# Sliding windows by DMA: twelve staged batches instead of eleven, direct copies in halves, a rebuilt end

## The chip, the cores and the metric

The kernel runs on one core of one Trainium2 chip. The metric is the device time of one execution in microseconds. The core has 16 DMA engines, which all its DMA queues share; the trace records every packet that they move, with its queue, size, start and duration.

## The reference

`x` has 32 batches of 4096 rows of 256 float32 values. Each batch is cut into windows of 64 rows, one every 32 rows, so 127 windows overlap by half:

```python
n_windows = (length - window_size) // stride + 1          # 127
result = np.zeros((batch, n_windows, window_size, dim), dtype=np.float32)
for i in range(n_windows):
    start = i * stride                                    # 32 * i
    result[:, i] = x[:, start:start + window_size].copy()
```

Nothing is computed, only copied: 134 MB in, 266 MB out. In units of a block (32 rows, 32 KB) a batch has 128 blocks, and window `w` is block `w` followed by block `w + 1`. Every block but the first and last of a batch is written twice.

## The kernel before, in words

All data is moved by DMA, on three queues. A batch goes one of two ways:

- **Direct** (21 batches): DRAM to DRAM. `Copier.windows` (L29) copies `n` windows; with `half=None` each window is one row of 64 KB, cut into pieces of at most 32 KB; with `half` 0 or 1 only the first or second block of each window is copied, one piece of 32 KB each. SyncE (SP, `ring_d`, queue q1 of the profile) issues them, 16 windows at a time, seven groups a batch.
- **Staged** (11 batches: 1, 4, 7, ... 31): `Staging.load` (L86) brings the 128 blocks of a batch into a tile of 128 partitions, 32 KB each, and `Staging.store` (L97) writes the tile out twice, once as the first halves of the windows and once as the second halves. ScalarE (ACT, `ring_s`, q10) issues them, in pieces of 16 KB. Six tiles are used in turn: six loads, then their twelve stores, then five loads that each wait for the tile's stores, then their stores (`run`, L116).

A staged batch's store writes all 128 blocks both times, so its first halves spill one block into the next batch's window 0, and its second halves one block into the window 126 of the batch before. Those windows belong to direct batches and are written again after the store has landed. These are the **edges** (L166): of the 127 windows of a direct batch, seven groups of 16 are 112, and the other 15, on the side of the staged neighbour, are left to GpSimd (POOL, `ring_r`, q0). POOL waits for the semaphore `near` (L192), which the group of q1 before the last one raises when it lands, then for the `stored` semaphore of each neighbour (L196), and issues the edges in order. The last staged batch, 31, is loaded one block early and stored in smaller parts (L103 to L110); the last direct batch, 30, ends with two `columns` DMAs (L200, L203) that cut windows into small rows spread over all engines.

What each queue gets is set ahead of time by a planner written into the loop (L171 to L187): it counts "turns" of the staged queue and sets, by stage, what share of the 16-window groups is issued as two halves and which as whole windows: 120 of 120 at the start and around the second loads, 90 of 120 while loads run, 18 of 120 otherwise. At the end SP waits for all semaphores (L206).

Each queue is a list in order: ACT's waits (tile free, tile loaded) hold back everything that ACT issues later, POOL's hold back later edges, and SP's later direct groups. The functions as they stand, with the profile's line numbers:

Of the kernel before, what the change touches and what calls it, by code (L numbers as in the profile page):

```python
# [8 lines left out]
DIRECT, IN, OUT = 32768, 16384, 16384  # L9


class Copier:


    def __init__(self, x, out, B, L, D, W, S, n_win):
        assert W == 2 * S and L % S == 0
        self.x, self.out = x, out
        self.B = B
        self.blk = S * D
        self.nb = L // S  # L20
        self.nw = n_win
# [18 lines left out]
    def columns(self, q, b, w0, n):  # L40
# [5 lines left out]
            in_=self.xap(b * self.nb + w0, [[part, 16], [self.blk, n], row]),  # L46
        )

    def load(self, q, t, b, c, rows):

        p, step, n, unit = rows
        return q.dma_start(
            out=t[p : p + (n - 1) * step + 1 : step, :],
            in_=self.xap(b * self.nb + c + p // unit, [[step // unit * self.blk, n], [1, self.blk]]),
            max_dma_last_dim=IN,
        )

    def store(self, q, t, b, c, rows, half):


        p, step, n, unit = rows
        w = b * self.nw + c + p // unit - half
        return q.dma_start(
            out=self.oap(2 * w + half, [[2 * step // unit * self.blk, n], [1, self.blk]]),
            in_=t[p : p + (n - 1) * step + 1 : step, :],
            max_dma_last_dim=OUT,
        )


class Staging:  # L70


    def __init__(self, c, tc, pool, dtype, items, bufs):
        self.c, self.items = c, items
        self.tiles = [pool.tile([128, c.blk], dtype, name=f"xb{i}") for i in range(bufs)]
        self.loaded = [tc.alloc_semaphore(f"loaded{i}") for i in range(bufs)]
        self.stored = [tc.alloc_semaphore(f"stored{i}") for i in range(bufs)]
        self.ended = tc.alloc_semaphore("ended")
        self.count = {sem: 0 for sem in (*self.loaded, *self.stored, self.ended)}
        self.after_load, self.after_store = {}, {}  # L80

    def issue(self, dma, sem):
# [2 lines left out]

    def load(self, q, g):  # L86
        i = g % len(self.tiles)
        b, c, n = self.items[g]
        if self.count[self.stored[i]]:
            q.wait_ge(self.stored[i], self.count[self.stored[i]])  # L90
        step = 128 // n
        parts = [(k, 4, 32, 1) for k in range(4)] if g == 0 else [(0, step, n, step)]
        for rows in parts:
            self.issue(self.c.load(q, self.tiles[i], b, c, rows), self.loaded[i])
        self.after_load[g] = self.count[self.loaded[i]]

    def store(self, q, g):  # L97
        i = g % len(self.tiles)
        b, c, n = self.items[g]
        q.wait_ge(self.loaded[i], self.after_load[g])  # L100
        step = 128 // n
        parts, end = [((0, step, n, step), 0), ((0, step, n, step), 1)], []
        if g == len(self.items) - 1:  # L103

            parts = [((0, 1, 128, 1), 1), ((0, 1, 32, 1), 0)]
            end = [(96, 1, 32, 1)] + [(32 + k, 4, 16, 1) for k in range(4)]
        for rows, half in parts:
            self.issue(self.c.store(q, self.tiles[i], b, c, rows, half), self.stored[i])
        for rows in end:
            self.issue(self.c.store(q, self.tiles[i], b, c, rows, 0), self.ended)  # L110
        self.after_store[g] = self.count[self.stored[i]]

    def wait_stored(self, q, g):
        q.wait_ge(self.stored[g % len(self.tiles)], self.after_store[g])  # L114
# [1 line left out]
    def run(self, q):  # L116
        bufs = len(self.tiles)
        for first in range(0, len(self.items), bufs):
            group = range(first, min(first + bufs, len(self.items)))
            for g in group:  # L120
                self.load(q, g)
            for g in group:
                self.store(q, g)


@with_exitstack
def kernel(
    ctx: ExitStack,
    tc: tile.TileContext,
    x: bass.AP,  # L130
    window_size: bass.AP,
    stride: bass.AP,
    out: bass.AP,
):
    nc = tc.nc
    W, S = int(window_size), int(stride)
    B, L, D = x.shape
    n_win = (L - W) // S + 1
    assert out.shape == (B, n_win, W, D)
    c = Copier(x, out, B, L, D, W, S, n_win)  # L140


    staged = [*range(1, B, 3)]
    items = [(b, -1 if b == B - 1 else 0, c.nb) for b in staged]
    place = {b: g for g, (b, _, n) in enumerate(items) if n == c.nb}
    direct = [b for b in range(B) if b not in staged]
    pool = ctx.enter_context(tc.tile_pool(name="xb", bufs=1))
    st = Staging(c, tc, pool, x.dtype, items, 6)
    ring_d, ring_s, ring_r = nc.sync, nc.scalar, nc.gpsimd
    done = tc.alloc_semaphore("done")  # L150
    near = tc.alloc_semaphore("near")
    rest = tc.alloc_semaphore("rest")
    total = {done: 0, near: 0, rest: 0}

    def count(dma, sem):
        dma.then_inc(sem, 16)
        total[sem] += 16

    sixteens = []
    for b in direct:
        w = 15 if b - 1 in staged else 0
        sixteens += [(b, w + 16 * j) for j in range((c.nw - w) // 16)]
    singles = [(B - 1, c.nw - 1, 1)]
    edges = [(b, 0 if b - 1 in staged else 112, 15) for b in direct[:-1]]  # L166
    last = B - 2
    edges.append((last, 112, 4))

    first_loads, loads, stores = 6 * 17, 5 * 17, 6 * 34  # L170
    turns = share = 0  # L171
    with tc.tile_critical():  # L172
        st.run(ring_s)

        for i, (b, w) in enumerate(sixteens):
            sem = near if i == len(sixteens) - 2 else done
            second = turns - first_loads - stores
            loading = turns < first_loads or 0 <= second < loads
            share += 120 if turns < 16 or -8 <= second < 16 else 90 if loading else 18
            if share >= 120:  # L180
                share -= 120
                turns += 4
                count(c.windows(ring_d, b, w, 16, 0), done)
                count(c.windows(ring_d, b, w, 16, 1), sem)
            else:
                turns += 3
                count(c.windows(ring_d, b, w, 16), sem)  # L187
            if i == len(sixteens) // 2:
                for b, w, half in singles:
                    count(c.windows(ring_d, b, w, 1, half, 2048), done)  # L190

        ring_r.wait_ge(near, 16)  # L192
        for b, w, n in edges:
            for k in (b - 1, b + 1):
                if k in place and b != last:
                    st.wait_stored(ring_r, place[k])  # L196
            count(c.windows(ring_r, b, w, n), rest)


        count(c.columns(ring_r, last, 116, 9), rest)  # L200
        ring_r.drain()  # L201
        st.wait_stored(ring_d, place[B - 1])
        count(c.columns(ring_d, last, 125, 2), done)  # L203
        total[st.ended] = st.count[st.ended]
        for sem, n in total.items():
            ring_d.wait_ge(sem, n)  # L206
# [35 lines left out]
```

## Time and profile before

| what | value |
|---|---|
| median of 3 runs | 754.74 us (751.68 to 755.06) |
| span of the profiled execution, first to last instruction | 742.1 us |
| bytes moved by the DMA engines | 313.26 MB, mean 422 GB/s |
| DMA packets | 18290, of these 4336 of 4 bytes (completions) |
| direct groups on SP | 92 of 1024 KB (whole windows), 110 of 512 KB (halves) |
| staged loads and stores on ACT | 10 loads and 21 stores of 4096 KB, and 10 smaller DMAs |
| POOL starts its first edge | at 649.1 us of the span |
| last DMA packet ends | at 739.7 us |

The profiled execution's own time is not listed apart from its span; the span lies 12.6 us below the median of the runs. Times in the text are in the span's clock. MB and GB/s of the DMA engines count a byte once when it is moved; HBM counts it when it is read and when it is written, so a direct copy is two HBM bytes a byte moved and a staged load or store is one. "Excess" is used for the time that packets take beyond the shortest time of their size.

### The profile page before, as it was taken

To read this page: it belongs to the slowest core of one execution; us is meant where nothing else is said; L and a number is where in the kernel's file an instruction comes from. 1 tells how busy PE (TensorE), PEld (TensorE's weight loads), DVE (VectorE), ACT (ScalarE), POOL (GpSimd) and SP (SyncE) were. 2 spreads that over 40 slices of the span, in tenths; PEclk is the share of its full clock that TensorE was granted. 3 is DMA by queue.
4 is the path that set the end of the run, shared out by engine and by line. 5 is a ranking of instruction groups with operands and counts; after the bars stand their busy time and mean duration, and the time that the engine had idled before them with its cause. 6 is when DMAs were issued, how large, how long until landed. Compare 5 with 4: busy or idle time off the path is not lost.

```text
span 742.1 us, 323 instructions
## 1 busy us (share of the span) xinstructions
POOL 12.7 (2%) x26
## 2 busy tenths in 40 slices
POOL 0000000000000000000000000000000000050100
DMA  8999999999999999999999999999999999999996
GB/s 361 424 430 427 435 431 428 423 435 425 428 427 426 428 428 420 429 435 427 427 427 412 433 435 431 427 436 432 434 424 429 430 424 426 428 435 432 421 420 253
DMA packets 18290, 313.26 MB, mean 422 GB/s; under 512 B 4336, under 2 KB 4336, under 8 KB 4528
## 3 DMA queue, kind: packets, MB, share of 16 engines
q1 hardware_dynamic: 8016, 154.32, 48.8%
q10 hardware_dynamic: 9104, 138.41, 44.0%
q0 software_dynamic: 1168, 20.51, 6.6%
q14 instruction: 2, 0.02, 0.0%
HBM read 220.95 MB, written 267.09 MB: 658 GB/s over the span
## 4 chain that ended last, share of the span: by engine, by line
another core or an unknown queue 92%; POOL 2%; issue 0%; POOLq 0%; SPq 0%
POOL out_dram L34 2%; POOLq L201 0%; POOLq L237 0%; SPq L172 0%; POOLq L114 0%
## 5 line engine op out<-in xcount | busy, mean ns | idle before, releaser
L34 POOL DMA_DIRECT2D out_dram<-in_x_dram x21 | 12.0, 575 | 685.4 <-DMA out_dram<-in_x_dram 648.7
L44 POOL DMA_DIRECT2D out_dram<-in_x_dram x1 | 0.6, 581 | 0.0
L223 POOL MEMSET const-float32-0.0<- 128x1 f32 x1 | 0.1, 98 | 0.2 <-issue 0.2
L223 POOL MEMSET const-bfloat16-1.0<- 128x1 bf16 x1 | 0.1, 101 | 0.0
L223 POOL MEMSET const-float32-1.0<- 128x1 f32 x1 | 0.1, 98 | 0.0
L223 POOL MEMSET const-uint8-127<- 128x1 uint8 x1 | 0.1, 98 | 0.0
## 6 DMA issues: line engine op xcount, KB each, us to landing
out_dram<-in_x_dram SPq DMA_DIRECT2D x92, 1024.0 KB, 99.8
out_dram<-xb ACTq DMA_DIRECT2D x21, 4096.0 KB, 138.5
out_dram<-in_x_dram SPq DMA_DIRECT2D x110, 512.0 KB, 90.2
xb<-in_x_dram ACTq DMA_DIRECT2D x10, 4096.0 KB, 130.5
out_dram<-in_x_dram POOLq DMA_DIRECT2D x20, 960.0 KB, 37.9
xb<-in_x_dram ACTq DMA_DIRECT2D x4, 1024.0 KB, 15.7
out_dram<-xb ACTq DMA_DIRECT2D x2, 1024.0 KB, 110.5
out_dram<-xb ACTq DMA_DIRECT2D x4, 512.0 KB, 94.4
```

Of the source, the lines that this page charges most:

```text
L34: return q.dma_start(out=self.oap((b * self.nw + w0) * 2 + h, [[2 * blk, n], row]), in_=self.xap(b * self.nb + w0 + h, [[blk, n], row]), m ...
L44: return q.dma_start(out=self.oap((b * self.nw + w0) * 2, [[part, 16], [2 * self.blk, n], row]), in_=self.xap(b * self.nb + w0, [[part, 16 ...
L223: nc = _bacc.Bacc("TRN2", target_bir_lowering=False, num_devices=1)
```

## The change

- Twelve batches are staged: 1, 4, ... 22, then 24, 26, 29 and 30. Batches 29 and 30 are neighbours, so each spills into the other. `store_pair` writes them together: first, under the semaphore `spilt`, the four half-tile stores that hold the spilled blocks, then one store to fill the wait, then, after `spilt`, the three that write over the spilled blocks.
- Every second staged batch is stored in DMAs of every other partition (`put` with `n = 2`), 64 blocks each.
- All direct groups are halves (512 KB, one piece of 32 KB a window); the planner is gone. Direct batches between two staged neighbours (23, 25) have an edge at each side.
- After the third group SP issues two `quarter` DMAs: 8 rows of 16 KB each, half a block of eight windows of batch 31.
- SP keeps back its last 16 halves until an edge near the end of POOL's list has landed (`back`), and two more, next to the pair, until `spilt`.
- POOL also issues, in the middle of its list, what is left of batch 31 at windows 96 to 119, and cuts every third edge into 16 KB pieces.

```diff
+    def quarter(self, q, b, w, n, k):
+        part = self.blk // 2
+        return q.dma_start(
+            out=bass.AP(self.out.tensor, self.out.offset + (b * self.nw + w) * 2 * self.blk + k * part, [[2 * self.blk, n], [1, part]]),
+            in_=bass.AP(self.x.tensor, self.x.offset + (b * self.nb + w) * self.blk + k * part, [[self.blk, n], [1, part]]),
+        )
...
+    def put(self, q, g, part, half, sem):
+        k, n = part
+        i = g % len(self.tiles)
+        self.issue(self.c.store(q, self.tiles[i], self.items[g], 0, (k, n, 128 // n, 1), half), sem)
...
-        for rows, half in parts:
-            self.issue(self.c.store(q, self.tiles[i], b, c, rows, half), self.stored[i])
-        for rows in end:
-            self.issue(self.c.store(q, self.tiles[i], b, c, rows, 0), self.ended)
+        for half in (0, 1):
+            n = 2 if (2 * g + half) % 4 < 2 else 1
+            for k in range(n):
+                self.put(q, g, (k, n), half, self.stored[i])
         self.after_store[g] = self.count[self.stored[i]]
+
+    def store_pair(self, q, g):
+        for k in (g, g + 1):
+            q.wait_ge(self.loaded[k % len(self.tiles)], self.after_load[k])
+        even, odd = (0, 2), (1, 2)
+        for k, part, half in ((g, even, 1), (g, odd, 0), (g + 1, odd, 0), (g + 1, even, 1)):
+            self.put(q, k, part, half, self.spilt)
+        self.put(q, g, even, 0, self.ended)
+        q.wait_ge(self.spilt, self.count[self.spilt])
+        for k, part, half in ((g + 1, even, 0), (g, odd, 1), (g + 1, odd, 1)):
+            self.put(q, k, part, half, self.ended)
...
-    staged = [*range(1, B, 3)]
+    staged = [1, 4, 7, 10, 13, 16, 19, 22, 24, 26, B - 3, B - 2]
+    alone = staged[:-2]
...
+    last, held = B - 1, 16
     for b in direct:
-        w = 15 if b - 1 in staged else 0
-        sixteens += [(b, w + 16 * j) for j in range((c.nw - w) // 16)]
+        first = 15 if b == last - 3 else 0 if b - 1 not in alone else 7 if b + 1 in alone else 15
+        sixteens += [(b, first + 16 * j) for j in range(7)]
+        if b != last:
+            edges += [(b, w, n) for w, n in ((0, first), (first + 112, 15 - first)) if n]
+    odd = -sum(n for _, _, n in edges) % 16
+    late = [e for e in edges if alone[-1] in (e[0] - 1, e[0] + 1)]
+    edges = [e for e in edges if e not in late] + late
+    halves = [(b, w, half) for b, w in sixteens for half in (0, 1)]
+    spoilt = [(last - 3, c.nw - 16, 1), (last, 0, 0)]
+    halves = [h for h in halves if h not in spoilt and h[:2] != (last, 96)]
+    middle, main = len(halves) // 2, len(halves) - held
...
-        for i, (b, w) in enumerate(sixteens):
...
-            share += 120 if turns < 16 or -8 <= second < 16 else 90 if loading else 18
...
+        blocks(halves[:3])
+        for k in (0, 1):
+            count(c.quarter(ring_d, last, 96, 8, k), done)
+        blocks(halves[3:middle])
+        count(c.columns(ring_d, last, 120 + odd, 7 - odd), done)
+        blocks(halves[middle : main - 5])
+        blocks(halves[main - 5 : main - 4], near)
+        blocks(halves[main - 4 : main])
 
         ring_r.wait_ge(near, 16)
-        for b, w, n in edges:
+        for i, (b, w, n) in enumerate(edges):
+            if i == 8:
+                count(c.windows(ring_r, last, 104, 8), rest)
+                count(c.windows(ring_r, last, 96, 8, 1, DIRECT // 2), rest)
+                for half in (0, 1):
+                    count(c.windows(ring_r, last, 112 + odd, 8, half, DIRECT // 2), rest)
+                count(c.windows(ring_r, last, 112, odd), rest)
             for k in (b - 1, b + 1):
-                if k in place and b != last:
+                if k in alone:
                     st.wait_stored(ring_r, place[k])
-            count(c.windows(ring_r, b, w, n), rest)
-        count(c.columns(ring_r, last, 116, 9), rest)
+            count(c.windows(ring_r, b, w, n, piece=DIRECT if i % 3 != 1 else DIRECT // 2), back if i == len(edges) - 4 else rest)
         ring_r.drain()
-        st.wait_stored(ring_d, place[B - 1])
-        count(c.columns(ring_d, last, 125, 2), done)
+        ring_d.wait_ge(back, 16)
+        blocks(halves[main:])
+        ring_d.wait_ge(st.spilt, st.count[st.spilt])
+        blocks(spoilt)
```

## The prediction

> **What bounds the kernel now.** I read the page from the top: busy time, slices, queues. One engine shows any work, POOL with 12.7 us, and the chain of waits puts 92% of the span on "another core or an unknown queue", which here can only be DMA. So the lines that carry the case are the DMA ones (busy share in tenths and GB/s by slice of 18.6 us; then each queue's packets, MB and share of the time of 16 DMA engines):
>
> ```profile
> DMA  8999999999999999999999999999999999999996
> GB/s 361 424 430 427 435 431 428 423 435 425 428 427 426 428 428 420 429 435 427 427 427 412 433 435 431 427 436 432 434 424 429 430 424 426 428 435 432 421 420 253
> ...
> q1 hardware_dynamic: 8016, 154.32, 48.8%
> q10 hardware_dynamic: 9104, 138.41, 44.0%
> q0 software_dynamic: 1168, 20.51, 6.6%
> ...
> HBM read 220.95 MB, written 267.09 MB: 658 GB/s over the span
> ```
>
> q1 is SP's queue (direct copies), q10 ACT's (staged batches), q0 POOL's (edges). 48.8 + 44.0 + 6.6 = 99.4%: the 16 DMA engines have no idle time outside the two ends. The kernel is bound by packet time, and every packet added or removed counts. The second view is the busy time by stretch, cut at the landings of the staged transfers: loads up to 132 us, stores to 407, loads to 511, stores to the end (columns: stretch, length, POOL, clock, DMA share, GB/s):
>
> ```profile
> 0.00:20.00 20.00, 0.20 (x4) 1.00 0.90 367
> 20.00:80.00 60.00, 0.00 (x0) 1.00 1.00 426
> 80.00:132.00 52.00, 0.00 (x0) 1.00 1.01 431
> 132.00:400.00 268.00, 0.00 (x0) 1.00 1.01 428
> 400.00:420.00 20.00, 0.00 (x0) 1.00 1.00 416
> 420.00:520.00 100.00, 0.00 (x0) 1.00 1.01 431
> 520.00:650.00 130.00, 0.89 (x2) 1.00 1.01 428
> ...
> 700.00:730.00 30.00, 0.00 (x0) 1.00 1.01 416
> 730.00:742.10 12.10, 0.00 (x0) 1.00 0.42 169
> ```
>
> 431 GB/s is the clean rate; the share stays at 1.0 where the rate is lower, so lower rates are longer packets, not pauses. The third source is the trace's records of single packets. Between one packet's start and the next on the same engine lie 1210 ns for 32 KB (recorded 1213), 607.5 ns for 16 KB (recorded 611), 156 ns for 4 KB, 81 ns for 2 KB and 6 ns for a completion packet of 4 bytes. Before has 5312, 8448, 176, 16 and 4336 of these: 6427.5 + 5132.2 + 27.5 + 1.3 + 26.0 = 11,614 us of one engine, over 16 engines **725.9 us**. The span is then: first packet at 2.4, plus 725.9, plus 7.5 that packets took beyond these times ("excess", summed over all data packets and divided by 16), which is 735.8 as the mean end of an engine; the last engine ends 3.9 later (739.7; the 0.42 share of the last row is this straggler); 2.4 of closing instructions. Sum 742.1. The median of the runs, 754.74, lies 12.6 us above this span, which I take as what surrounds it and keep.
>
> **The change, part by part.**
>
> *A twelfth staged batch.* Output bytes are the same, but the batch's 4.19 MB pass the DMA engines once more as a load: 256 packets of 16 KB, 256 x 607.5 / 16 = +9.7 us. Since the engines are full, nothing hides it. Counting every issue of the changed code gives 4448 + 410 = 4858 packets of 32 KB on q1 and q0, 9216 + 412 + 16 = 9644 of 16 KB, 64 of 4 KB and, with 16 a DMA and POOL's surplus as now, 5808 completions. Against before: 32 KB -454 x 1210 = -34.3; 16 KB +1196 x 607.5 = +45.4; 4 and 2 KB -1.2; completions +1472 x 6 = +0.6. Together **+10.5, so 736.4 us** of pure packet time. That is 317.5 MB against 313.2.
>
> *All direct blocks as halves of 512 KB, the planner of shares gone.* Cost: the completions above. Gain: it can reduce the 7.5 us of excess. By stretch it is 0.89 (0 to 20 us), 0.62 (to 80), 0.20 (to 132), 2.47 (to 400), 0.60 (to 420), 0.01 (to 520), 1.08 (to 650), 0.26 (to 700), 1.40 (to the end). The queues take turns packet by packet, completions included, so whole windows give q1 64 KB in 3 turns and halves 64 KB in 4. In the store stretches, mostly whole windows, q1 and q0 moved 1.30 to 1.33 times q10's bytes; in the load stretches, mostly halves, 1.15. After, it should be 1.06 (32 KB in 2 turns against sixteen 16 KB in 17) to 1.13 (against eight in 9) throughout, 8.4 of 16 engines on direct packets instead of 9.0 to 9.4 in the store stretches. Pieces of 5 us from the two store stretches, sorted by engines on direct packets, show an excess of 0.7 ns a us (7 to 8 engines), 5.0 (8 to 9), 9.7 (9 to 10), 29 (over 10). After has some 440 us of store stretches ahead of its tail: I take the middle row, 5.0, for 2.2 us; the ends are 0.7 (0.3 us) and 9.7 (4.3 us).
>
> *Quarters, half a turn.* Two DMAs of 8 rows of 16 KB give engines 0 to 7 two packets (1.2 us, half of the 2.4 us that a direct 32 KB and two staged 16 KB take), made up for by a smaller share at q0's end. It spreads the direct packets: in the first 80 us the number of engines on them swings from 0 to 16 (standard deviation 4.8 to 5.9), at 420 to 520 us by 2.3. What it can save is the 0.62 of 20 to 80 us and part of the head; below nothing it could cost the same if the groups met again. For head, both load stretches and the step between stages I take 0.7 + 0.3 + 0.6 = 1.6 (ends 0.8 and 2.3).
>
> *Edges, held halves, the pair.* q1's main part has 260 data packets an engine, as many completions and one small DMA: 525 turns, beside q10's 576 + 53 = 629. POOL starts some 9 turns ahead of q1's end, when the store of batch 24 has about landed; batches 19 and 22 landed earlier, so its waits are already met. POOL has about 77 turns; `back` lands near its 70th, with q10 at some 587. Behind SP's wait stand 18 halves (9.4 MB, 36 turns) beside q10's last 40: they end together. SP's issues, 0.66 us each (44 in 29.24 us at the start), outrun the 2.3 us that a half needs, and q0's three last edges (1.97 MB) cover the restart. ACT's wait for `spilt` has one 2.1 MB store queued ahead of it, some 10 us at q10's 210 GB/s. If covers fail, the others' packets fill the engines; the price is a direct-only end, below. For the tail's excess I take 0.5 (ends 0.3 and 1.4, the last row now).
>
> *The straggler.* Engines with equal bytes drift apart: the slowest completion of a q1 DMA came 0.8 us behind the first at 50 us, 2.3 at 400, 4.1 at 635. With half the excess I take 2.4 us from mean to last instead of 3.9 (ends 1.3 and 4.0).
>
> **Sum.** 2.4 + 736.4 + (2.2 + 1.6 + 0.5 = 4.3) + 2.4 + 2.4 = 747.9 us of span, with 12.6 around it **760.5**, 5.8 us or 0.8% above the median. The change buys back some 5 of the 10.5 us it spends. All low ends: 741.2 + 1.4 + 1.3 = 743.9, so 756.5. All high ends: 741.2 + 8.0 + 4.0 = 753.2, so 765.8.
>
> The count of DMAs costs little by the trace: the 512 KB issues of before move in the cleanest stretch (431 GB/s, three quarters of its direct blocks halves), so I price a further DMA at 16 completions of 6 ns. [...]
>
> **The rivals.**
>
> *Clean copy (24%).* An even number of direct packets leaves excess only at the head, as from 420 to 520 us (0.01), and the engines stay together: the low ends, 756.5 to 757.5, +0.3%: no change. For it: 100 us without excess, at a ratio of 1.15. Against it: that was a load stretch; no store stretch was clean, and the bursts stand at ends of stores, of which there are now more.
>
> *Memory-bound (4%), faster.* If HBM and not the DMA engines set the rate, staging pays: HBM bytes fall from 488.0 to 483.9 MB (a direct batch is read as 8.3 MB, a staged one as 4.2), at the profile's 658 GB/s -6.3 us: 748.4. It decides from the point where packets lengthen as the engines fill with direct work. Against it: at that rate packets take their shortest time but for 1%, so 6.3 us would be nearly all the excess there is, and the added packets cost 10.5. [...]
>
> *Nothing bought back (12%), slower still.* With one fixed turn on all queues the engines can lock in step, as in the first 80 us, and excess and straggler stay at 7.5 and 3.9; or q10 ends before the held halves and up to 9.4 MB run alone, 32 accesses at once. At 658 GB/s of HBM that is 28.6 instead of 21.8 us, +6.8. Both give about 765.
>
> *The forecast (60%)*: 758 to 763.5.
>
> A measurement of this kernel tells about 0.5% (3.8 us) from no change. Faster by more needs a span under 738.4, below the 741.2 of packets alone: only the memory-bound case, 4%. Within 0.5%: the clean copy and a little of the forecast, 26%. Slower: 70%. The range from 756.5 to 765.8 takes in both ends of the costs and all but the memory-bound case.
>
> **What would show it.** Right: 317.5 MB, q10 at 151 MB and about 48% share, HBM read near 217 MB; store stretches at 429 to 431 GB/s; last slice fuller than 253. Half a turn: rows from 20 to 80 us at 430 instead of 426. Wrong: a span under 741 (packets shorter than their minimum), a dip in the last 40 us with share near 1 (direct packets alone) or with share below 1 (held back too long), or store stretches at 425.

## The result and the profile after

The changed kernel took 758.38 us (median of 14 runs, 755.48 to 760.26) and the kernel before 754.33 beside it: ratio 1.0046, 95% interval 1.0028 to 1.0064. The profiled execution has a span of 756.5 us for a time of 758.25. The page after, in the lines that were shown of before:

```profile
DMA  8999999999999999999999999999999999999995
GB/s 362 422 432 425 432 431 423 432 430 428 431 436 424 425 431 430 428 431 430 420 429 432 429 430 431 433 432 431 425 431 424 429 428 431 427 416 416 413 400 196
...
q10 hardware_dynamic: 10064, 151.00, 47.0%
q1 hardware_dynamic: 9008, 146.29, 45.8%
q0 software_dynamic: 1472, 20.19, 6.5%
...
HBM read 216.79 MB, written 267.12 MB: 640 GB/s over the span
```

The engines are as full as before (99.3%). More slices stand at 431 or above, but the last six fall from 427 to 196, where before kept 420 up to its last one. By stretch (columns as before: stretch, length, POOL, clock, DMA share, GB/s):

```profile
20.00:132.00 112.00, 0.00 (x0) 1.00 1.01 428
132.00:400.00 268.00, 0.00 (x0) 1.00 1.01 429
400.00:520.00 120.00, 0.00 (x0) 1.00 1.01 431
520.00:640.00 120.00, 13.12 (x23) 1.00 1.00 428
...
680.00:720.00 40.00, 0.00 (x0) 1.00 1.01 420
720.00:740.00 20.00, 0.00 (x0) 1.00 1.01 386
740.00:756.50 16.50, 0.00 (x0) 1.00 0.50 174
```

From 720 to 740 us the share is 1.01 at 386 GB/s: no engine waits, but most direct packets are long (the median of 32 KB is 1453 ns). What runs there is seen in the timeline of issues and in SP's waits (longest wait last):

```profile
712.65 15.25 SPq L34 DMA_DIRECT2D out_dram<-in_x_dram  x18
```

```profile
SPq L34 <- DMA out_dram<-in_x_dram: 170.9, 1, 170.9
```

SP waits 171 us for `back` and issues the 16 held halves and the two spoilt ones from 712.7 us on, and by the packet records q10 has all but ended by 731. What is left is direct work alone, 32 KB packets of mostly 1400 to 1550 ns.

One number of the prediction's frame was wrong. 756.5 of span for 758.25 of time leaves 1.8 us around a span, not 12.6. The experiments point to the reason: before takes 744 us on some chips and 753 to 754 on others. The span of 742.1 in the profile of before fits a time of 744, while the timed runs took 754, so the two must have come from different chips. (Each chip was used in one session, so a chip and its session can't be told apart.) Below, each run is compared with before on its own chip, and runs of different chips only by their ratios to before, unless it is said otherwise. The ledger of the prediction (first packet + pure packet time + excess + straggle, which is the mean end of an engine to the last one, + closing) from four profiles:

| us | before, chip of 744 | changed, chip of 744 | before, chip of 753 | changed, chip of 754 |
|---|---|---|---|---|
| first packet | 2.4 | 2.4 | 2.4 | 2.4 |
| packets | 725.9 | 736.4 | 725.9 | 736.4 |
| excess | 7.5 | 6.1 | 17.0 | 10.0 |
| straggle | 2.8 | 5.3 | 2.4 | 6.0 |
| closing | 2.4 | 1.6 | 2.4 | 1.7 |
| span | 741.1 | 751.9 | 750.1 | 756.5 |

(Columns: e1, e5, e11, and the profile after.) Each column is one execution; e1 and e5 ran on different chips of 744, and the chip of the profile after is not known, so the 6.4 us between the last two spans is not the effect of the change, which is 4.05 us. The packets cost 10.5 us on either. In these profiles the change gets 7.0 us back as excess on the slower chips and 1.4 on the others, and on both the straggler takes some 3 us more.

### The profile page after: what moved, and what is told of

The parts are those of the page before. It is cut to its first block, busy times and chain, and to the rows that moved or that the text cites. A ratio compares the mean times of both kernels' runs of the same rounds, so it can differ in the third digit from the quotient of the medians.

```text
span 756.5 us, 421 instructions
## 1 busy us (share of the span) xinstructions
POOL 15.0 (2%) x30
## 2 busy tenths in 40 slices
DMA packets 20546, 317.50 MB, mean 420 GB/s; under 512 B 5978, under 2 KB 5978, under 8 KB 6042
## 3 DMA queue, kind: packets, MB, share of 16 engines
q10 hardware_dynamic: 10064, 151.00, 47.0%
q0 software_dynamic: 1472, 20.19, 6.5%
HBM read 216.79 MB, written 267.12 MB: 640 GB/s over the span
## 4 chain that ended last, share of the span: by engine, by line
another core or an unknown queue 85%; POOL 2%; issue 0%; POOLq 0%; SPq 0%
POOL out_dram L34 2%; POOLq L226 0%; POOLq L132 0%; POOLq L265 0%; SPq L202 0%
## 5 line engine op out<-in xcount | busy, mean ns | idle before, releaser
L34 POOL DMA_DIRECT2D out_dram<-in_x_dram x26 | 14.8, 574 | 646.9 <-DMA out_dram<-in_x_dram 615.2
```

What stands on the lines that cost most here:

```text
L34: return q.dma_start(out=self.oap((b * self.nw + w0) * 2 + h, [[2 * blk, n], row]), in_=self.xap(b * self.nb + w0 + h, [[blk, n], row]), m ...
```

## The experiments

Excess by stretch, which most of them turn on, in us (worked out from the packet records as in the prediction). Below, "ratio of direct to staged bytes" is what q1 and q0 move for each byte that q10 moves, and "ns a us" is the excess of an engine in a microsecond of its time:

| run | 0-20 | 20-130 | 130-390 | 390-520 | 520-620 | 620-700 | from 700 |
|---|---|---|---|---|---|---|---|
| e1, before | 0.95 | 0.99 | 2.35 | 0.79 | 0.80 | 0.49 | 1.17 |
| e5, changed | 0.64 | 0.61 | 0.50 | 0.06 | 0.04 | 0.95 | 3.35 |
| e2, earlier release | 0.67 | 0.64 | 0.55 | 0.12 | 0.04 | 1.61 | 2.19 |
| e3, no hold | 0.59 | 0.45 | 0.64 | 0.07 | 0.17 | 4.69 | 0.46 |
| e4, no early shift | 0.68 | 0.39 | 0.47 | 0.10 | 0.04 | 1.43 | 2.66 |
| e7, whole windows | 1.04 | 3.93 | 7.08 | 4.77 | 1.78 | 1.50 | 2.07 |
| e8, even share | 1.10 | 2.21 | 0.80 | 2.15 | 0.49 | 0.23 | 1.66 |
| e12, before in halves | 0.75 | 0.38 | 0.54 | 0.10 | 0.04 | 5.21 | 11.76 |
| e11, before, slower chip | 0.69 | 2.48 | 5.88 | 2.13 | 2.14 | 1.96 | 1.66 |
| changed, slower chip | 0.66 | 1.06 | 1.49 | 0.17 | 0.62 | 1.74 | 4.28 |

**e1: before again** (no edit).

> The kernel before, unchanged, to see an execution of it beside its time. Theory: the profiled execution of before (span 742.1) was some 10 us shorter than its usual ones, since the runs of the changed kernel lie only 1.8 us above their span (758.25 for 756.5); then a new profile has a span near 752.5, with the same 313.2 MB and the same packet counts, and the 10 us stand as longer packets or a later straggler. Rival: what surrounds the span is 12.6 us for this kernel; then the span is again near 742.

Measured: 743.45 us and a span of 741.1, where before took 744.09 in the runs beside it (ratio 0.9991, 0.9981 to 1.0). Neither theory as put: the span is again near 742, as the rival has it, but so is the time; what surrounds the span is 1.7 us. The 10 us lie between chips, or between their sessions.

**e5: the changed kernel again** (no edit), on a chip where before takes 743.9.

> The changed kernel, unchanged, beside the kernel before on one chip. Chips differ: before took 754.3 us where the change was measured and 744.1 on the chip of the first experiments. Theory (packet sum): on the chip where before takes 744 the changed kernel takes 753 to 756, 1.2 to 1.6% more, since its packets alone need 10.5 us more and its end wastes what the middle saves; on a chip where before takes 754 the difference is 4 us, because the excess of before is larger there. Rival: the difference is 4 us on every chip; then 748 where before is 744.

754.00 us, ratio 1.0132 (1.0119 to 1.0145). The packet sum held: 10.1 us more here, 4 on the slower chip. By the ledger the excess gave 1.4 us back and the straggler took 2.5, so the time stays near the packets' 10.5.

```profile
20.00:132.00 112.00, 0.00 (x0) 1.00 1.01 429
132.00:400.00 268.00, 0.00 (x0) 1.00 1.01 431
400.00:520.00 120.00, 0.00 (x0) 1.00 1.01 432
520.00:640.00 120.00, 13.18 (x23) 1.00 1.01 430
...
720.00:740.00 20.00, 0.00 (x0) 1.00 1.00 376
```

Up to 640 us it is clean but for the head and the start of the stores; 4.3 of its 6.1 us of excess come after 620.

**e11: before on a slower chip** (no edit; the runs of before beside it took 753.27).

> The kernel before once more, for its profile on this chip. Where before takes about 744, the ledger is that of the first experiment (excess 7.5, straggle 2.8). Should this chip be one on which before takes 754, then theory: the 10 us are excess in direct packets and straggle, and the changed kernel, with fewer direct bytes beside staged ones, loses less there; rival: packets of all kinds are longer by the same share.

751.89 us, span 750.1. Compare its stretches with 428 GB/s from 132 to 400 and 431 from 420 to 520 us in the first profile of before:

```profile
132.00:400.00 268.00, 0.00 (x0) 1.00 1.01 422
...
420.00:520.00 100.00, 0.00 (x0) 1.00 1.01 427
520.00:650.00 130.00, 0.00 (x0) 1.00 1.00 422
```

The excess is 17.0 instead of 7.5 us, most of it in the store stretches with their larger direct share; the shortest packets are as short as ever (1210 ns a packet of 32 KB, 607.5 of 16 KB). It is not in direct packets alone, as the theory has it: packets of 32 KB have 8.8 us of it and those of 16 KB 8.1, against 4.1 and 3.4 in e1, so by kind the rival is nearer. The straggle is not part of it (2.4), which that theory also held. Why one chip stretches packets more than another is open.

**e6: the twelfth load alone**, on before.

```diff
             for g in group:
                 self.load(q, g)
+            if first:
+                q.wait_ge(self.stored[5], self.count[self.stored[5]])
+                self.issue(self.c.load(q, self.tiles[5], 0, 0, (0, 1, 128, 1)), self.ended)
```

> The kernel before with a sixth load in the second stage, 4.19 MB into the sixth tile, which nothing stores: the bytes of a twelfth staged batch's load and nothing else of the change. Packet sum: 256 packets of 16 KB, 607.5 ns each, over 16 engines: +9.7 us, to 753 to 754.5 where before takes 744. Rival of the memory's limit: the load is one HBM access a byte and dilutes the direct copies beside it, so it costs under 5 us.

755.05 us (752.07 to 757.33), 11 us or a ratio of 1.0146 (1.0128 to 1.0164) above before; its profile has 9.2 us more span than e1 (on another chip of 744), with 735.6 us of packets and 7.4 of excess. q10 moves 142.61 MB instead of 138.41:

```profile
q10 hardware_dynamic: 9376, 142.61, 44.9%
```

The load costs its packet time in full; the memory's limit does not pay for it.

**e12: the halves alone**, on before.

```diff
-            share += 120 if turns < 16 or -8 <= second < 16 else 90 if loading else 18
+            share += 120 if turns < 16 or -8 <= second < 16 else 120
```

> The kernel before, eleven staged batches, with all direct groups as halves (the planner's share at 120 throughout): the halves of the change without its twelfth batch. Theory of the ratio: q1 and q0 then move about 1.06 times q10's bytes, 8.3 engines on direct packets, and from 130 to 390 us the excess falls from 2.35 to about 0.5 us (from 5.9 to about 1.5 on a chip where before takes 754); but q10 then ends with some 25 MB of direct work left, which alone moves at 350 instead of 430 GB/s: 13 to 15 us lost at the end, so that the time rises by 8 to 12 us on a chip where before takes 744. Rival: the lower excess came with the twelfth batch or the new stores, and halves alone leave it above 2 us from 130 to 390.

758.47 us, ratio 1.0193 (1.0176 to 1.021): 14 us, more than the 8 to 12 expected.

```profile
132.00:400.00 268.00, 0.00 (x0) 1.00 1.01 431
...
640.00:680.00 40.00, 0.00 (x0) 1.00 1.01 406
680.00:720.00 40.00, 12.54 (x22) 1.00 0.88 299
720.00:740.00 20.00, 0.00 (x0) 1.00 1.01 339
```

Excess from 130 to 390 us is 0.54, as in the changed kernel: the halves clean the middle, not the twelfth batch nor the stores in two parts. But q10 ends at 676 us, and direct work alone moves 339 GB/s with all engines busy; the rest of the 14 us is in the main a gap (share 0.88, 4.7 us of the mean engine's time) between the end of q1 and POOL's first edges. So this is what the twelfth batch is for: it gives q10 enough to last beside halves.

**e7: whole windows**, on the changed kernel: `blocks` joins two neighbouring halves into one DMA.

```diff
+        part = list(part)
+        while part:
+            b, w, half = part.pop(0)
+            if half == 0 and part and part[0] == (b, w, 1):
+                part.pop(0)
+                half = None
             count(c.windows(ring_d, b, w, 16, half), sem)
```

> The changed kernel with SP's neighbouring halves joined to whole windows (64 KB a window in two pieces) wherever both follow each other, so that q1 moves 32 KB in 1.5 turns instead of 2. Theory of the ratio: the share of direct bytes rises to 1.33 to 1.4 of q10's, the store stretches get their excess back (about 9 ns a us, 2 us or more from 140 to 400), while the direct work ends early and staged stores run alone at the end: the excess moves rather than grows, 752 to 757. Rival: what cleaned the store stretches is the store's own new form (every other partition), not the ratio; then they stay at 0.02 us per 20 us.

765.72 us, far over the 752 to 757 expected, ratio 1.0288 (1.0275 to 1.0302).

```profile
20.00:132.00 112.00, 0.00 (x0) 1.00 1.00 416
132.00:400.00 268.00, 0.00 (x0) 1.00 1.01 420
400.00:520.00 120.00, 0.00 (x0) 1.00 1.01 416
```

The ratio of direct to staged bytes is 1.40 to 1.43 here, and excess comes back everywhere, 22.2 us in all; the stores keep their new form, so that form is not what cleans them. The ratio fits the excess, but it changes together with the number of whole windows; that the ratio decides, and not the two packets of a window one behind the other, is not shown. The excess grew rather than moved, against the expectation.

**e8: one even share**, on before.

```diff
-            share += 120 if turns < 16 or -8 <= second < 16 else 90 if loading else 18
+            share += 120 if turns < 16 or -8 <= second < 16 else 41
```

> The kernel before with its planner's share set to 41 of 120 in load and store stretches alike (90 and 18 before), so that the ratio is about 1.25 throughout. Theory: excess grows faster than the ratio, so one even ratio has less of it: from 7.5 to some 6.5 us, and the time falls by 0.5 to 1.5 us. Rival: store stretches need a ratio near 1.1 to be clean, and 1.25 spoils the load stretches as well: the time stays or rises by up to 2 us.

743.53 us beside 743.93, ratio 0.9999 (0.9986 to 1.0012): no change. The ratio is 1.26 to 1.29 throughout, and excess moves from the stores to the loads (in all 8.6 us against 7.5):

```profile
20.00:132.00 112.00, 0.00 (x0) 1.00 1.00 423
132.00:400.00 268.00, 0.00 (x0) 1.00 1.01 431
400.00:520.00 120.00, 0.00 (x0) 1.00 1.01 424
```

At one ratio the loads are now the slow stretches (20 ns a us, stores 3). So in this run direct copies disturb loads sooner than stores, and the planner of before leaned the right way. With e5, e1 and e7 this gives a row by ratio: at 1.06 to 1.08 hardly any excess; stores 3 ns a us at 1.26, 9 at 1.34, 27 at 1.43; loads 20 at 1.28, 36 at 1.40. All these are chips of 744; on the slower ones stores have 6 ns a us at 1.07 (the profile after) and 23 at 1.34 (e11).

**e4: the shift undone**, on the changed kernel: the two quarters are issued after SP's main part.

```diff
-        for k in (0, 1):
-            count(c.quarter(ring_d, last, 96, 8, k), done)
...
         blocks(halves[main - 4 : main])
+        for k in (0, 1):
+            count(c.quarter(ring_d, last, 96, 8, k), done)
```

> The changed kernel with its two quarter DMAs issued after the main part of SP's list instead of after the third group, so that engines 0 to 7 are not shifted at the start. If the shift does what it says, the number of engines on direct packets swings between 0 and 16 in the first 80 us (standard deviation about 5 instead of 2.1 to 2.6), with an excess of 0.5 to 1 us more there, and the time rises by 0.5 to 2 us. Rival: the shift saves nothing (20 to 80 us had 0.64 us of excess with it and 0.62 in the profile of before without it); then the time is the same within 0.5 us.

753.64 us beside before at 744.09; the changed kernel took 754.00 beside 743.93 on another chip (e5). The ratios 1.0128 (1.0109 to 1.0146) and 1.0132 overlap: nothing gained by the shift.

```profile
20.00:132.00 112.00, 0.00 (x0) 1.00 1.01 430
132.00:400.00 268.00, 0.00 (x0) 1.00 1.01 431
```

The shift does do what it says. In the profile after, the 16 packets of the two quarters start eight by eight, from 10.2 to 10.7 us and again 1.83 to 1.89 us later: eight engines, two packets each. Without it the number of engines on direct packets swings from 0 to 16 up to 620 us (standard deviation about 6). With it the deviation from 20 to 620 us is 1.5 to 2.5 in the profile after, but 3.2 to 4.5 in e5, so the shift does not hold in every execution. All that swinging costs nothing here: 0.47 us of excess from 130 to 390, with it 0.50. So in this pair of runs it did not matter how many engines go direct at once; that the mean over many turns is what counts is a reading of it, not shown by itself.

**e2 and e3: the held halves earlier, and not held**, on the changed kernel.

```diff
-... back if i == len(edges) - 4 else rest)
+... back if i == len(edges) - 9 else rest)      # e2
...
-        ring_d.wait_ge(back, 16)                   # e3
```

> The changed kernel with SP's 16 held halves released by an edge five places earlier in POOL's list. Theory: in the changed kernel the held halves come too late, since POOL's queue needs more turns than counted, so that q10 ends some 20 us ahead of q1, and direct packets alone take about 1500 ns instead of 1213; released earlier, the excess after 700 us falls from 4.3 to about 1 us, no stretch of direct packets alone remains, and the time falls by 4 to 7 us to 752 to 754. Rival: the end is set by one straggling engine, whatever the order; then the time stays within 1.5 us of 758.4.

> The changed kernel with SP's 16 halves issued at once, without the wait for back. Theory of the late release: q1, q0 and q10 run three abreast after 615 us, some 11 engines on direct packets, with excess there but no direct-only end; the last 15 to 25 us are staged stores alone at full rate: 752 to 756. Rival of the memory's limit: three abreast is as bad as direct-only, the excess of 3 to 5 us only moves forward, and the time stays at 757 to 760.

753.33 and 754.26 us beside before at 744.09: ratios 1.0121 (1.0103 to 1.0139) and 1.0136 (1.0118 to 1.0154). The times fall into both theories' bands only because this is a chip of 744; held against e5's ratio, 1.0132, neither gained. e2, then e3:

```profile
680.00:720.00 40.00, 0.00 (x0) 1.00 1.01 405
720.00:740.00 20.00, 0.00 (x0) 1.00 1.01 422
```

```profile
615.00:680.00 65.00, 11.56 (x22) 1.00 1.00 402
680.00:720.00 40.00, 1.02 (x2) 1.00 1.01 426
```

The dip from 720 to 740 us is gone and stands elsewhere: where q1, q0 and q10 run three abreast, some 11 engines on direct packets. After 620 us the excess is 3.8 and 5.2 us, with the hold 4.3. The theory of the late release falls: in these two places the excess moves with the held halves. That no other place would be better is not shown. After 615 us there are 1.22 to 1.25 direct bytes to a staged one, which at the 3 ns a us of e8's stores, if kept even, would cost some 0.4 us in 135 (an estimate); but e5 has 12 ns a us from 620 to 700 us, where q0 is the direct queue, at a ratio of only 1.03, and no run explains that.

**e9 and e10: edges with even bytes**, POOL's windows as `columns` of 16 x 4 KB pieces, on the changed kernel (also without quarters, and with the middle of POOL's list cut the same way) and on before.

```diff
-            count(c.windows(ring_r, b, w, n, ...), ...)
+            count(c.columns(ring_r, b, w, n), ...)
```

> The changed kernel without the quarters and with every DMA of POOL cut into 16 columns of 4 KB pieces, so that each of them gives all 16 engines the same bytes; in the changed kernel POOL's DMAs of 15, 8, 7 and 3 windows reach only some engines each. Theory of uneven edges: the last engine ends 5.3 to 6.0 us after the mean because of what POOL's queue gives it; with even columns the straggle falls to 1 to 2 us, at a cost of some 2 us for 4 KB packets (156 ns for 4 KB against 1210 for 32 KB), and the time falls by 1 to 3 us below the 754.0 of the changed kernel. Rival: the straggler is an engine that lost time to long packets; then it stays at 5 to 6 us and the time rises by 1 to 2 us.

> The kernel before with POOL's edges as 16 columns of 4 KB pieces, nothing else changed. Theory of uneven edges: straggle of 2.8 to 3.8 us falls to 1 to 2, packets cost 1.5 us more, and the end has 4 KB pieces to interleave: 742.5 to 744.5 where before takes 743.9. Rival of the longest packets: straggle stays near 3 and the time rises to 745 or 746.

767.47 and 766.32 us beside before at 753.27, ratios 1.0189 (1.0175 to 1.0203) and 1.0191 (1.017 to 1.0212). The changed kernel itself was not run on this chip. Both theories missed why. In e9:

```profile
660.00:700.00 40.00, 0.00 (x0) 1.00 1.01 400
700.00:730.00 30.00, 0.00 (x0) 1.00 0.96 323
730.00:765.00 35.00, 0.00 (x0) 1.00 0.83 278
```

With one packet a turn (in the profile after, q0 and q10 have 618 and 616 records from 640 to 680 us), 4 KB packets let POOL's queue move about a quarter of what q10's 16 KB do, an estimate from those counts. q10 ends at 692 us, and 70 us of direct work alone follow. On the straggler e9 decides nothing. Its last engine ends 5.8 us after the mean by the ledger, but 4.1 of these are engines idle from 700 to 740 us, while SP waited for `back` (it issues its held halves from 731.5 on):

```profile
730.00:734.00 4.00, 0.00 (x0) 1.00 0.54 183
```

After that the engines start together again, and at the end 2.1 us are lost (counted from the packets in flight). In e12, which has such a gap and POOL's uneven edges, it is 2.3. e10 has hardly a gap and 4.6 us with even bytes, against 2.4 in e11, which speaks against uneven edges as the cause. The records do not name a packet's engine, so who lags and why stays open.

## Why the prediction was right, and where it was not

- **Packet sum, +10.5 us: right.** 317.50 MB and 736.4 us of packets; e6 shows the main term alone, forecast as 9.7: 9.2 us by the spans, 11 by the times.
- **Excess bought back by the even ratio: right in kind.** Forecast 4.3 us in all; measured 6.1 on the chips the working was made for, 10.0 on the slower one. The middle was cleaner than taken (stores from 130 to 390 us at 0.50 / 260 = 1.9 ns a us against 5.0; on the slower chip 5.7), the tail far dirtier: 4.3 us after 620 against 0.5.
- **The turns: right for q1 and q10.** 1.05 to 1.08 times q10's bytes, against 1.06 to 1.13. The counts of records show the turns: from 132 to 400 us q1 has 3180 and q10 3181 in the profile of before, 3691 and 3694 in the profile after. The measured ratios fit a turn of one record, of 16 or 32 KB or a completion.
- **"They end together": the step that failed.** POOL's queue was to start 9 turns ahead of q1's end, and `back` to land near its 70th turn with q10 at 587 of its 629. In the packet records of the profile after, q0's first packet comes with half a turn of q1's main part left and q10 at 530, some 14 turns later than counted. The first held half comes at q0's last turn, where 7 were to be left, with q10 at 617. q0 was counted at 77 turns an engine; it has 1472 packets / 16 = 92, since 650 of them are completions and not 16 for each of its 26 DMAs. So 9.5 MB of direct work stood beside 2.6 MB of staged work, and some 7 MB of it ran alone. POOL's wait of 31.7 us for the store of batch 26, which the working leaves out, cost nothing: q0 never paused for more than 3.1. The two earlier releases, e2 and e3, did not mend the time.
- **The straggler, 2.4 us: mis-sized.** 5.3 and 6.0; it is not in proportion to the excess, and its cause is open.
- **"12.6 around it": wrong**, it is 1.8. This put some 11 us too much on the time, and the slower chip, whose span was 8.7 us over the forecast 747.9 (758.38 - 1.8 = 756.6), put most of it back. That 760.5 lies so close to 758.38 is luck. On a chip of 744, like that of the first profile, the span was 751.9, 4.0 over the forecast.
- **Half a turn: no gain**, of the small one allowed (e4).
- **Slower by over 0.5%, at 70%:** 0.46% (0.28 to 0.64) where the change was measured, under that mark; 1.3% on the one other chip where the changed kernel was run (e5), and 1.2 to 1.4% for its variants on a third (e2 to e4).
- **Its own signs.** 317.50 MB, q10's 151.00 MB, 216.79 MB of HBM reads and 429 GB/s in the store stretch came as forecast. The last slice was emptier (196 against 253), and the dip near the end with a share near 1, named as a sign of being wrong, came (386 GB/s from 720 to 740 us).
- **Rivals.** Clean copy: true up to 620 us on a chip of 744, and undone by the end. Memory-bound: e6 rules it out as the general limit. It may be the limit where direct work is alone, where 339 GB/s moved (e12) are 678 read and written, but no run shows that. Nothing bought back: its direct-only end came (3.35 us of excess after 700), its price of 6.8 did not in full. In sum it is the nearest on a chip of 744, where the time rose by 10.1 of the 10.5 us, against the forecast's 5.8.

No version tried beats the kernel before by more than its interval; on a chip of 744 the changed kernel's packets, first packet and closing alone (736.4 + 2.4 + 1.6 = 740.4) leave 0.7 us below the span of before, less than either kernel's straggle.

## What to carry to other kernels

Where DMA engines are full, count packets first: added bytes cost their packet time (here 9.7 us counted, 9.2 measured by the spans in e6), and a better mix can give back only the excess that is there (7.5 us in e1, 17.0 in e11), which a trace shows as the difference between packets and their shortest time. Here the mix was set by what each queue moves in a turn, completions included (3691 records of q1 beside 3694 of q10 from 132 to 400 us), so count the turns of every queue from its packets before planning what ends with what. Profile and time on the same chip before the two are subtracted from each other: here that was the 10.8 us between 12.6 and 1.8.

## What the runs showed of the hardware

The same kernel took 744 us on three chips (e1, e5, e12) and 753 to 754 in the measurement of the change and on the chip of e11, with the same shortest packets: 32 KB at 1210 ns a packet, 16 KB at 607.5. DRAM-to-DRAM copies alone take 1400 to 1600 ns for 32 KB on all 16 engines, 339 GB/s in e12. Beside staged traffic, on chips of 744 and up to 620 us, they run at nearly full speed (429 to 432 GB/s) at a byte ratio of about 1.1, even when all 16 engines go direct at the same moment (e4). With more of them loads suffer sooner than stores (e8: 20 against 3 ns a us near 1.27).
